# Modulation of layer 2 and both layers' output gates: from TensorE rows to VectorE products with running sums

## Chip, cores and metric

The kernel runs on one core of one Trainium2 chip. The metric is the device time of one execution in microseconds (us), as the median of three runs. TensorE (PE) multiplies matrices into PSUM banks, VectorE (DVE) and ScalarE (ACT) work on them and on SBUF, GpSimd (POOL) does some additions, and SyncE (SP) issues all DMAs. Each engine runs its instructions in the order in which the program lists them.

## What is computed

Two layers of a mixer with shared weights for 128 context tokens and 512 latent tokens, 640 rows of 1024 columns in all. The conditioning vectors (one for each token group) give a shift, a scale and a gate per layer:

```python
for l in range(DEPTH):                                   # DEPTH = 2
    sh, sc, gt = split(silu(c) @ w_mod[l] + b_mod[l], 3) # c_ctx or c; w_mod[l] is 1024 x 3072
    h = rmsnorm(x, pre_w) * (1 + sc) + sh
    proj = h @ w_in                                      # z, xbc, dt | q, k, v, g_b | u, sv, g_c | mg
    y_a = ssd_mixer(...)       # conv, softplus(dt), chunked scans both ways, gated norm
    y_b = diff_attention(...)  # two softmax maps per head
    y_c = chunk_sgmlp(u, sv) * silu(g_c)
    merged = ga * (y_a @ w_branch[0]) + gb * (y_b @ w_branch[1]) + gc * (y_c @ w_branch[2])
    x = x + gt * rmsnorm(merged @ w_out, post_w)
```

## The kernel before

**Dense products.** Every weight matrix is cut into column units. A unit of kind "F" is 128 output columns against all 640 tokens in two halves of 320 (`dense_F`, L532 to L534); a unit of kind "T" is 352, 256 or 512 output columns against five tiles of 128 tokens (`dense_T`, L472 to L474). Both operands are split into a rounded high part and a low part, and three products (high·high, high·low, low·high) are added in PSUM. A weight chunk of 128x1024 is loaded raw by SP (L388), rounded by ACT (L410), and its low part is made by DVE (L419).

**Order.** `schedule()` lists the units of both layers. In each layer come v and gate columns with q and k (attention runs beside them), then mgb (gate of branch b), brb (branch b) mixed with the three sv units, u and gc, two xbc units, mgc and brc in turn, xbc with z (the scans run beside them), mga, bra, and wo (output). All other work is written as small generators. A clock of ticks, one for every six dense products or so, decides when the next piece of each generator is written into the program, so the order on every engine is fixed when the kernel is built. A generator's `yield 3` means "three ticks later".

**PSUM.** Dense halves and tiles take banks of group "d": banks 0 and 1, and, from the end of attention until wo, bank 6 as well. A bank comes free when its result has been read: by ACT for the mg units (L1583), by DVE for brb (L1104), brc (L1107) and bra (L1112), and by a chain ACT, DVE L1020, ACT, DVE L1024 for sv and u.

**Modulation.** Units of kind "M" multiply the conditioning vectors with w_mod: one unit is half of the 1024 rows and 512 columns, four products side by side on 32 columns each (`mod_part`, L666), with the raw weights as the moving operand, in plain float32. There are 24 of them: 8 at the start (scale and shift of layer 1), 8 between the brb units of layer 1 (scale and shift of layer 2), and 4 in bra of each layer (gates, blocks 4 and 5). After two halves `mod_post` adds the bias (L674). Scale and shift are turned into columns by four small products (L683) and finished by L687 and L689. A gate is spread over all 128 partitions by two products with a selecting matrix (L698), and multiplied with the post-norm weight (L700) into `gp`, which `wo_evac` reads (L1467). The post-norm row is spread by a DMA (L661), the bias row loaded by another (L650) into a tile that POOL clears (L649).

**Softplus.** `softplus` (L1168 to L1187) is written in one piece: two ACT instructions and then 18 DVE instructions without a gap, once per layer, while brb ends and u begins.

Of the kernel before, what the change touches and what calls it, by code (L numbers as in the profile page):

```python
# [6 lines left out]
F32 = mybir.dt.float32  # L7
# [3 lines left out]
ALU = mybir.AluOpType  # L11
# [17 lines left out]
D_MOD0, D_MOD, D_GATE = (1, 1), (5, 4), (5, 6)  # L29
D_GAP = (0, 0, 1)  # L30
D_X = (1, 3, 5, 7, 9, 26)
D_MLOAD = 3
# [8 lines left out]
NCOL = 81  # L41
C_PRE, C_CW, C_CB, C_MN, C_DF, C_DB, C_VN, C_HN = 0, 8, 38, 48, 56, 64, 72, 80
# [7 lines left out]
def schedule():  # L50
# [4 lines left out]
    for l in range(DEPTH):  # L55
# [7 lines left out]
        mgb, brb = [("F", "mgb", l, d, 128) for d in range(8)], []  # L63
        for d in range(8):
            brb.append([("F", "brb", l, d, 128)] + ([("M", d % 2, l + 1, d // 2, 512)] if l + 1 < DEPTH else []))
# [8 lines left out]
        for d in range(8):  # L74
            u.append(("F", "mgc", l, d, 128))
            u.append(("F", "brc", l, d, 128))
        for f in range(8):
# [153 lines left out]
class Build:  # L231
    def __init__(self, ctx, tc, a, mem):
        self.a = a
        self.mem = mem
        if tc is None:
            self.nc = self.P = self.PR = self.x1 = Null()
            self.csd = self.ecd = [Null()] * DEPTH
            self.V, self.R, self.I = ([Null()] * 4 for _ in range(3))
        else:
# [14 lines left out]
            self.ecd = [dr.tile([32, 512], F32, name=f"ecd{l}") for l in range(DEPTH)]  # L254
        self.free = [6, 7]
# [8 lines left out]
        for ui, k, kk in chunk_order(self.units):  # L264
            sz = kk * self.units[ui][4]
            self.cid[ui].append(len(self.chunks))
            self.chunks.append((off, sz, self.units[ui][0] == "M"))
# [125 lines left out]
    def mod_load(self, ui):  # L393

        for u in range(ui, min(ui + D_MLOAD + 1, len(self.units))):
            if self.units[u][0] == "M":
# [3 lines left out]
                return  # L400
# [238 lines left out]
    def mod_unit(self, ui):  # L639
        if self.units[ui][1] == 0:  # L640
            self.force(lambda: any(self.group[b] == "s" for b in self.free))
            self.mod_bank = next(b for b in self.free if self.group[b] == "s")
            self.free.remove(self.mod_bank)
        self.mod_part(ui, self.mod_bank)
        self.tick()

# [5 lines left out]
    def mod_part(self, ui, b):  # L652
# [3 lines left out]
        if half == 0:  # L656
            if l or blk >= 4:
                self.mod_bias(l, blk)
            if blk == 4:
                self.pw = self.al(1024)  # L660
                nc.sync.dma_start(out=self.v(self.pw), in_=self.a["postw"][l:l + 1, :].to_broadcast([128, 1024]))  # L661
# [7 lines left out]
        if half:  # L669
            self.go(self.mod_post(l, blk, b, self.rb.pop((l, blk)), D_MOD if l else D_MOD0 if blk < 4 else D_GATE))  # L670

    def mod_post(self, l, blk, b, rb, D):
# [5 lines left out]
        if blk < 4:  # L678
            if l not in self.pm:
                self.pm[l], self.sh[l] = self.al(16), self.al(16)  # L680
            t = (yield from self.take("t")) if l else 5
            for j in range(4):
                nc.tensor.matmul(self.P[:, t, 2 * j:2 * j + 2], self.v(rb, 128 * j, 128), self.msel, start=True, stop=True)  # L683
            yield D[1]
            dst = self.v(self.pm[l], 4 * blk, 4)
            pre = self.v(self.cols[l], C_PRE + 2 * blk, 2).unsqueeze(2).to_broadcast([128, 2, 2])
            nc.vector.scalar_tensor_tensor(out=dst.rearrange("p (j c) -> p j c", j=2), in0=self.P[:, t, 0:4].rearrange("p (j c) -> p j c", j=2),  # L687
                                           scalar=1.0, in1=pre, op0=ALU.add, op1=ALU.mult)
            nc.vector.tensor_copy(self.v(self.sh[l], 4 * blk, 4), self.P[:, t, 4:8])  # L689
            if l or blk == 3:  # L690
                self.give(t)
        else:
            if blk == 4:
                self.gp = self.al(2048)
# [1120 lines left out]
```

## Time and profile before

| what | value |
|---|---|
| median of 3 runs | 2236.98 us (2236.21 to 2237.16) |
| the profiled execution: time, span | 2239.7 us, 2237.7 us |
| PE busy | 2195.2 us, 98% of the span |
| DVE busy | 1371.5 us, 61% |
| ACT busy | 1022.2 us, 46% |
| DMA | 244.05 MB, mean 109 GB/s |
| granted TensorE clock, mean | 0.993 |

The profiled execution is one execution, 2.7 us above the median of the runs. Durations below are from it. Matmul ends are modelled in the profile and matmuls overlap, so what one product costs PE is read from the distance of the starts around it. In the first layer, the units from sv to the last brb stand at 444 to 559 us, u and gc at 560 to 675 us, mgc and brc at about 690 to 804 us, bra at 1023 to 1078 us.

### The profile page before, as it was taken

What the parts mean: (1) busy time and instruction counts of PE and PEld (TensorE: products, weight loads), DVE (VectorE), ACT (ScalarE), POOL (GpSimd) and SP (SyncE); (2) the same over time, 40 slices, a digit from 0 to 9 for tenths busy, and PEclk for the clock granted to TensorE, in tenths of its full rate; (3) what the DMA queues carried; (4) which work ended last, traced back from release to release, by engine and by line L of the source; (5) the groups of instructions that cost most, each with busy time, mean ns of one, the idle gap of its engine ahead of it and who ended that gap; (6) DMA issues with size and microseconds to landing.
All of it is one profiled execution on the core that took longest, in us unless ns stands there. A gap on an engine that the chain in (4) does not pass through costs nothing.

```text
span 2237.7 us, 38780 instructions
## 1 busy us (share of the span) xinstructions
PE 2195.2 (98%) x15482; PEld 2106.5 (94%) x15482; DVE 1371.5 (61%) x2597; ACT 1022.2 (46%) x2242; POOL 186.0 (8%) x196
## 2 busy tenths in 40 slices
PE   7999999999999999999989999999999999999998
PEld 4999999999999999998869999999999999999986
DVE  5476677536554259976375767774464532899654
ACT  4465566432333246762264655564323322677421
POOL 1000000000010113320000000000001011132100
PEclk9999999999999999999999999999999999999999
DMA  8333333234123134633233333322221231545251
GB/s 299 109 100 97 88 102 100 95 116 160 57 77 115 57 104 141 167 118 133 103 128 109 104 88 100 92 81 72 92 81 62 76 116 43 164 132 156 92 189 47
DMA packets 94380, 244.05 MB, mean 109 GB/s; under 512 B 13868, under 2 KB 27244, under 8 KB 94200
## 3 DMA queue, kind: packets, MB, share of 16 engines
q1 hardware_dynamic: 94200, 241.59, 34.5%
q8 instruction: 121, 1.98, 0.4%
q14 instruction: 59, 0.48, 0.1%
HBM read 206.64 MB, written 8.68 MB: 96 GB/s over the span
## 4 chain that ended last, share of the span: by engine, by line
PE 84%; DVE 8%; ACT 4%; issue 2%; DMA 2%; SPq 0%; DVEq 0%; ACTq 0%
PE psum L533 19%; PE psum L534 18%; PE psum L532 18%; PE psum L472 5%; PE psum L473 5%; PE psum L474 5%; PE psum L909 3%; PE psum L956 3%; PE psum L939 1%; PE psum L666 1%; PE psum L1078 1%; ACT plain L923 1%; ACT rounded L410 1%; PE psum L1335 1%; DMA plain<-csd 1%
## 5 line engine op out<-in xcount | busy, mean ns | idle before, releaser
L533 PE MATMUL psum<-shared,rounded 128*128 128x320 f32 x3136 | 972.1, 310 | 4.7 <-DVE shared L1052 4.7
L532 PE MATMUL psum<-shared,rounded 128*128 128x320 f32 x3136 | 973.5, 310 | 0.4 <-DVE plain L1024 0.4
L534 PE MATMUL psum<-shared,rounded 128*128 128x320 f32 x3136 | 965.0, 308 | 0.0
L532 PEld LDWEIGHTS psum<-shared,rounded 128*128 128x128 f32 x3136 | 591.6, 189 | 17.8 <-issue 13.5
L533 PEld LDWEIGHTS psum<-shared,rounded 128*128 128x128 f32 x3136 | 589.8, 188 | 7.2 <-DVE shared L1052 6.1
L534 PEld LDWEIGHTS psum<-shared,rounded 128*128 128x128 f32 x3136 | 591.4, 189 | 0.0
L419 DVE TENSOR_TENSOR rounded<-plain,rounded 128x1024 fp32r<-128x1024 f32 (+2 forms) x226 | 280.1, 1240 | 201.7 <-ACT rounded L410 197.1
L410 ACT CAST rounded<-plain 128x1024 fp32r<-128x1024 f32 (+2 forms) x226 | 235.7, 1045 | 204.3 <-PE psum L533 192.3
L472 PE MATMUL psum<-rounded,shared 128*128 128x256 f32 (+2 forms) x920 | 297.9, 324 | 5.8 <-DVE plain L821 5.8
L473 PE MATMUL psum<-rounded,shared 128*128 128x256 f32 (+2 forms) x920 | 291.7, 317 | 0.2 <-DVE rounded L419 0.2
L474 PE MATMUL psum<-rounded,shared 128*128 128x256 f32 (+2 forms) x920 | 290.9, 316 | 0.9 <-DVE shared L796 0.9
L472 PEld LDWEIGHTS psum<-rounded,shared 128*128 128x128 f32 x920 | 173.4, 188 | 18.7 <-DVE plain L821 7.4
L474 PEld LDWEIGHTS psum<-rounded,shared 128*128 128x128 f32 x920 | 173.5, 189 | 10.6 <-DVE shared L796 1.5
L473 PEld LDWEIGHTS psum<-rounded,shared 128*128 128x128 f32 x920 | 173.4, 188 | 9.5 <-DVE rounded L419 0.9
L917 DVE TENSOR_REDUCE plain<-psum 128x1 f32<-128x640 f32 (+1 forms) x160 | 107.7, 713 | 87.2 <-PE psum L909 86.1
L923 ACT ACTIVATE plain<-psum,plain 128x640 f32<-128x640 f32 (+1 forms) x160 | 112.3, 711 | 4.1 <-DVE plain L917 2.7
L909 PE MATMUL psum<-shared 128*128 128x320 f32 (+1 forms) x576 | 99.8, 312 | 0.0
L1583 ACT ACTIVATE plain<-psum 128x320 f32<-128x320 f32 x96 | 41.6, 436 | 123.3 <-PE psum L534 117.7
L962 ACT ACTIVATE plain<-psum,plain 128x128 f32<-128x128 f32 x80 | 29.6, 370 | 135.3 <-PE psum L956 96.4
L1018 ACT ACTIVATE plain<-psum 128x320 f32<-128x320 f32 (+1 forms) x62 | 27.7, 447 | 128.1 <-PE psum L534 65.2
L909 PEld LDWEIGHTS psum<-shared 128*128 128x128 f32 x576 | 84.6, 189 | 0.7 <-ACT plain L923 0.4
L956 PE MATMUL psum<-plain 128*128 128x128 f32 x640 | 81.3, 274 | 0.0
(268 smaller groups left out, 2558.0 us busy)
## 6 DMA issues: line engine op xcount, KB each, us to landing
plain<-in_wp_dram SPq DMA_DIRECT2D x250, 512.0 KB, 4.3
shared<-in_wp_dram SPq DMA_DIRECT2D x42, 512.0 KB, 6.4
shared<-csd SPq DMA_DIRECT2D x36, 320.0 KB, 5.2
shared<-shared SPq DMA_DIRECT2D x64, 160.0 KB, 3.1
plain<-csd SPq DMA_DIRECT2D x28, 320.0 KB, 7.1
plain<-plain SPq DMA_DIRECT2D x128, 64.0 KB, 2.0
plain<-in_wp_dram SPq DMA_DIRECT2D x12, 528.0 KB, 7.4
shared<-shared SPq DMA_DIRECT2D x32, 192.0 KB, 2.6
```

The lines of the kernel that those rows point to most:

```text
L410: self.nc.scalar.copy(self.r(blk[0], 0, sz), self.v(self.w_raw[i], 0, sz))
L419: self.nc.vector.tensor_tensor(out=self.r(blk[1], 0, sz), in0=self.v(raw, 0, sz), in1=self.v(blk[0], 0, sz), op=ALU.subtract)
L472: mm(out, ht, wh, start=(k == 0), stop=False)
L473: mm(out, ht, wl, start=False, stop=False)
L474: mm(out, lt, wh, start=False, stop=(k == KD - 1))
L532: mm(out, wh, xh, start=(k == 0), stop=False)
L533: mm(out, wh, xl, start=False, stop=False)
L534: mm(out, wl, xh, start=False, stop=(k == KD - 1))
L909: mm(self.P[:, ss[m] + half, 0:n], self.r(H["q"], 1280 * i + 640 * m + 128 * t, 128), k, start=(i == 0), stop=(i == 1))
L917: nc.vector.tensor_reduce(out=self.v(st, m, 1), in_=src[m], op=ALU.max, axis=AX.XY if t else AX.X, negate=True)
L923: nc.scalar.activation(pv, src[m], AF.Exp, bias=self.v(st, m, 1), accum_out=self.v(st, 2 + m, 1))
L956: mm(out, self.v(wt, 128 * j, 128), self.v(H["v"], 128 * ((j + 1) % 5), 128), start=(j == 0), stop=(j == 4))
```

## The change

Eight M units at the start stay. The 16 others go, with their bias rows, the small products L683 of layer 2, the spreading products L698 and the postw row. In their place stand 32 units of kind "V", all of them in layer 1 of the program: each is one tile of 128 columns of w_mod, **transposed**, so that a partition is an output column and the 1024 inputs lie along the row. `mod_tile` multiplies the tile with the conditioning row, spread over the partitions, once for each of the two vectors, as a DVE scalar_tensor_tensor of 128x1024 that also writes the sum of the row (`accum_out`). 12 of the 32 are placed between the second brb and the first u unit, 20 among the mgc and brc units. V units load one tile of 512 KB each through SP, ahead of the unit before or the one before that. The bytes of w_mod loaded are the same.

`cond_rows` loads and spreads the two conditioning rows once (2 x 512 KB) and applies the SiLU: two ACT and two DVE instructions of 128x1024. `mod_end` adds the bias, forms 1+scale and gate times post-norm weight on tiles of 16 to 48 columns, transposes the 16 gate columns of each layer on PE, and writes them to DRAM. `gate_rows` reads them back, spread over 128 partitions (2 x 512 KB per layer), two bra units ahead of wo. The softplus gets gaps of one or two ticks between its steps.

```diff
-        for d in range(8):
-            brb.append([("F", "brb", l, d, 128)] + ([("M", d % 2, l + 1, d // 2, 512)] if l + 1 < DEPTH else []))
+        brb = [[("F", "brb", l, d, 128)] for d in range(8)]
+        vs = [("V", "mod", v // 24, v % 24, 128) for v in range(16, 48)] if l == 0 else []
...
+        for lo, hi, part in ((len(u) - 16, len(u), vs[V_N:]), (start + V_AT, names.index("u", start), vs[:V_N])):
+            for j, v in reversed(list(enumerate(part))):
+                u.insert(lo + (j + 1) * (hi - lo) // len(part), v)
...
             u.append(("F", "bra", l, d, 128))
-            if 3 <= d <= 6:
-                u.append(("M", (d - 3) % 2, l, 4 + (d - 3) // 2, 512))
...
+    def cond_rows(self):
...
+        for c in range(2):
+            nc.sync.dma_start(out=self.v(cb, 1024 * c, 1024), in_=self.a["crow"][c:c + 1, :].to_broadcast([128, 1024]))
...
+            nc.scalar.activation(self.v(th), x, AF.Tanh, scale=0.5)
+            yield 3
+            nc.vector.scalar_tensor_tensor(out=x, in0=self.v(th), scalar=1.0, in1=x, op0=ALU.add, op1=ALU.mult)
...
+    def mod_tile(self, ui):
...
+        yield from self.until(lambda: self.condok)
+        jb = self.al(1024)
+        for c in range(2):
+            nc.vector.scalar_tensor_tensor(out=self.v(jb if c == 0 else wb), in0=self.v(wb), scalar=1.0, in1=self.v(self.cb, 1024 * c, 1024),
+                                           op0=ALU.mult, op1=ALU.mult, accum_out=self.v(self.mc[l], 2 * i + c, 1))
+            if c == 0:
+                self.fr(jb)
+                yield 3
...
+            nc.tensor.transpose(self.P[0:16, t, 0:128], self.v(gt), self.ident)
...
+            nc.sync.dma_start(out=self.gd[l].rearrange("c (j n) -> (c j) n", n=128), in_=self.v(gr, 0, 128, 0, 16))
...
+    def gate_rows(self, l):
+        self.gp = self.al(2048)
+        for c in range(2):
+            self.nc.sync.dma_start(out=self.v(self.gp, 1024 * c, 1024), in_=self.gd[l][c:c + 1, :].to_broadcast([128, 1024]))
...
         nc.vector.tensor_scalar(d, e, 2.0, None, op0=ALU.add)
+        yield 2
         nc.vector.reciprocal(d, d)
+        yield 1
...
         for c in (11, 9, 7, 5, 3):
+            yield 1
             nc.vector.tensor_tensor(out=p, in0=p, in1=s, op=ALU.mult)
...
         while self.units[ui][1] != "wo":
+            if self.units[ui][3] == 6:
+                self.gate_rows(l)
             run_unit(ui)
...
-        self.force(lambda: self.mods[l] >= {4, 5})
```

The order of the instructions shows it at three places. On PE, between the fourth brb unit of layer 1 (L534 ends it) and the third sv unit (L472 begins it), the kernel before has a half M unit, four products on 32 columns:

```order
L533 MATMUL psum<-shared_398,rounded 128x320
L534 MATMUL psum<-shared_398,rounded 128x320
L666 MATMUL psum<-plain 32x512 x4
L472 MATMUL psum<-rounded,shared_65 128x352
L473 MATMUL psum<-rounded,shared_65 128x352
```

and the changed kernel, where the same three dense lines are L537 to L539 and L477 to L479, has

```order
L538 MATMUL psum<-shared_400,rounded 128x320
L539 MATMUL psum<-shared_400,rounded 128x320
L477 MATMUL psum<-rounded,shared_65 128x352
L478 MATMUL psum<-rounded,shared_65 128x352
L479 MATMUL psum<-rounded,shared_65 128x352
```

The M products are gone and nothing stands in their place. The same holds at all 16 units, 4 groups of L683 and 8 products L698, and apart from the two transposes L744 no other product on PE has changed its place among the dense ones.

On DVE, while brb 5 of layer 1 is computed (L1061 begins the layer norm of sv, L1104 frees a bank of brb, L419 is a weight's low part, the 128x5 rows are the norm's inverse root), the kernel before has

```order
L549 TENSOR_SCALAR plain<-plain 128x5
L556 TENSOR_TENSOR plain<-plain 128x5
L559 TENSOR_TENSOR plain<-plain 128x5
L562 SCALAR_TENSOR_TENSOR plain<-plain 128x5
L1104 SCALAR_TENSOR_TENSOR plain<-plain,psum 128x320
L556 TENSOR_TENSOR plain<-plain 128x5
```

and the changed kernel, where they are L554 to L567, L1156 and L424, has

```order
L711 SCALAR_TENSOR_TENSOR plain<-plain 128x1024 x2
L424 TENSOR_TENSOR rounded<-plain,rounded 128x1024
L1113 TENSOR_SCALAR plain<-plain 128x5
L552 TENSOR_SCALAR plain<-plain 128x5
L553 TENSOR_SCALAR plain<-plain 128x5
L554 TENSOR_SCALAR plain<-plain 128x5
L561 TENSOR_TENSOR plain<-plain 128x5
L711 SCALAR_TENSOR_TENSOR plain<-plain 128x1024 x2
L564 TENSOR_TENSOR plain<-plain 128x5
L1156 SCALAR_TENSOR_TENSOR plain<-plain,psum 128x320
```

Four products with sums (L711) now stand ahead of the instruction that frees the first bank of brb 5.

On SP, in bra of layer 1, the kernel before loads bias rows, the post-norm row and gate weights between the last branch weights and the input rows (L1453):

```order
L388 DMA plain<-in_wp_dram 128x1024 x9
L650 DMA plain<-in_bmod_dram 1x512
L661 DMA plain<-in_postw_dram 128x1024
L388 DMA plain<-in_wp_dram 128x1024 x6
L650 DMA plain<-in_bmod_dram 1x512
L388 DMA plain<-in_wp_dram 128x1024 x4
L1453 DMA plain<-in_xin_dram 128x1024 x5
```

and the changed kernel, where they are L393 and L1509, has

```order
L393 DMA plain<-in_wp_dram 128x1024 x9
L758 DMA plain<-gd_73 128x1024 x2
L393 DMA plain<-in_wp_dram 128x1024 x2
L1509 DMA plain<-in_xin_dram 128x1024 x5
```

The two gate rows (L758) take the place of eleven loads, and stand ahead of the last weights and the input rows.

## Rows read from the trace of the kernel before

**Rows 1.** The page, part 1: busy time, share of span, instructions

```profile
PE 2195.2 (98%) x15482; PEld 2106.5 (94%) x15482; DVE 1371.5 (61%) x2597; ACT 1022.2 (46%) x2242; POOL 186.0 (8%) x196
```

**Rows 2.** Timeline of PE around an M unit and L683: start, us, instruction

```profile
534.76 0.31 PE L534 MATMUL psum<-shared,rounded 128*128 128x320 f32 x1
535.00 1.06 PE L666 MATMUL psum<-plain 128*32 128x512 f32 x8
...
536.25 0.31 PE L533 MATMUL psum<-shared,rounded 128*128 128x320 f32 x1
...
540.32 0.31 PE L534 MATMUL psum<-shared,rounded 128*128 128x320 f32 x1
540.47 0.95 PE L683 MATMUL psum<-plain 128*128 128x2 f32 x8
...
541.51 0.30 PE L533 MATMUL psum<-shared,rounded 128*128 128x320 f32 x1
```

**Rows 3.** Timeline of PE around a spreading product L698 in bra

```profile
1056.08 0.31 PE L534 MATMUL psum<-shared,rounded 128*128 128x320 f32 x1
1056.23 1.02 PE L698 MATMUL psum<-plain 128*128 128x512 f32 x2
...
1057.23 0.31 PE L533 MATMUL psum<-shared,rounded 128*128 128x320 f32 x1
```

**Rows 4.** Lines L666, L683, L698 after 400 us: records, duration ns min/median/max

```profile
L666 PE MATMUL psum<-plain x128: 592/605/618, 434.6 to 2164.8; 128*32 128x512 f32 x128
L683 PE MATMUL psum<-plain x32: 165/251/251, 448.7 to 558.4; 128*128 128x2 f32 x32
L698 PE MATMUL psum<-plain x16: 592/593/593, 1056.2 to 2173.7; 128*128 128x512 f32 x16
```

**Rows 5.** Timeline of PE around two transposes of 128x128

```profile
697.62 0.31 PE L534 MATMUL psum<-shared,rounded 128*128 128x320 f32 x1
697.76 0.27 PE L1218 MATMUL psum<-plain 128*128 128x128 f32 x1
...
698.13 0.31 PE L533 MATMUL psum<-shared,rounded 128*128 128x320 f32 x1
```

**Rows 6.** Busy us by stretch: PE, PEld, DVE, ACT, POOL; clock, DMA share, GB/s

```profile
690.00:804.00 114.00, 114.00 (x792) 113.36 (x791) 35.46 (x43) 25.25 (x40) 12.45 (x15) 1.00 0.22 76
499.50:558.60 59.10, 59.10 (x403) 54.95 (x400) 36.07 (x79) 12.73 (x21) 3.83 (x3) 1.00 0.42 151
```

**Rows 7.** DVE instructions by shape: busy us, mean ns; idle before

```profile
L419 DVE TENSOR_TENSOR rounded<-plain,rounded 128x1024 fp32r<-128x1024 f32 x208 | 259.7, 1250 | 194.4 <-ACT rounded L410 189.9 <-DMA plain<-in_wp_dram 4.5
L930 DVE SCALAR_TENSOR_TENSOR plain<-plain 128x640 f32<-128x640 f32 x64 | 56.7, 885 | 2.3
L1481 DVE SCALAR_TENSOR_TENSOR plain<-plain 128x1024 f32<-128x1024 f32 x9 | 11.6, 1285 | 0.3
L1476 DVE TENSOR_SCALAR plain<-plain 128x1 f32<-128x1 f32 x10 | 1.5, 154 | 0.3
```

**Rows 8.** DVE instructions by shape, 499 to 560 us

```profile
L1535 DVE BATCH_NORM_STATS2 plain<-plain 128x6 f32<-128x512 f32 x10 | 6.4, 681 | 0.0
```

**Rows 9.** Timeline of DVE: two sv tiles, two brc units

```profile
480.61 0.52 DVE L1020 SCALAR_TENSOR_TENSOR plain<-plain,psum 128x352 f32<-128x352 f32 x1 [2.23 <-ACT plain L1018]
...
484.46 0.52 DVE L1020 SCALAR_TENSOR_TENSOR plain<-plain,psum 128x352 f32<-128x352 f32 x1 [2.24 <-ACT plain L1018]
...
745.21 0.49 DVE L1107 SCALAR_TENSOR_TENSOR plain<-plain,psum 128x320 f32<-128x320 f32 x1 [0.83 <-PE psum L534]
...
759.07 0.49 DVE L1107 SCALAR_TENSOR_TENSOR plain<-plain,psum 128x320 f32<-128x320 f32 x1 [0.83 <-PE psum L534]
```

**Rows 10.** The page, part 6, DMA issues: count, KB each, median us to landing

```profile
plain<-in_wp_dram SPq DMA_DIRECT2D x250, 512.0 KB, 4.3
...
plain<-in_xin_dram SPq DMA_DIRECT2D x7, 512.0 KB, 8.8
```

**Rows 11.** Timeline of PE in layer 2, behind the softplus

```profile
1664.31 0.42 PE L532 MATMUL psum<-shared,rounded 128*128 128x320 f32 x1 [0.44 <-DVE plain L1024]
```

More of the change, by code (lines that the diff above doesn't have):

```diff
@@ L254, in __init__ @@
             self.ecd = [dr.tile([32, 512], F32, name=f"ecd{l}") for l in range(DEPTH)]
+            self.gd = [dr.tile([2, DM], F32, name=f"gd{l}") for l in range(DEPTH)]
         self.free = [6, 7]
@@ L266, in __init__ @@
             self.cid[ui].append(len(self.chunks))
-            self.chunks.append((off, sz, self.units[ui][0] == "M"))
+            self.chunks.append((off, sz, self.units[ui][0] in ("M", "V")))
             off += 128 * sz
@@ L677, in mod_post @@
         yield D[0]
[L678 to L694, printed above, removed]
-            o = 512 * (blk - 4)
-            for c in range(2):
-                t = yield from self.take("t")
-                nc.tensor.matmul(self.P[:, t, :], self.gsel[c], self.v(rb), start=True, stop=True)
-                yield 3
-                nc.vector.tensor_tensor(out=self.v(self.gp, 1024 * c + o, 512), in0=self.P[:, t, :],
-                                        in1=self.v(self.pw, o, 512), op=ALU.mult)
-                self.give(t)
-            if blk == 5:
-                self.fr(self.pw)
@@ new lines, in mod_post @@
+        if l not in self.pm:
+            self.pm[l], self.sh[l] = self.al(16), self.al(16)
+        t = 5
+        for j in range(4):
+            nc.tensor.matmul(self.P[:, t, 2 * j:2 * j + 2], self.v(rb, 128 * j, 128), self.msel, start=True, stop=True)
+        yield D[1]
+        dst = self.v(self.pm[l], 4 * blk, 4)
+        pre = self.v(self.cols[l], C_PRE + 2 * blk, 2).unsqueeze(2).to_broadcast([128, 2, 2])
+        nc.vector.scalar_tensor_tensor(out=dst.rearrange("p (j c) -> p j c", j=2), in0=self.P[:, t, 0:4].rearrange("p (j c) -> p j c", j=2),
+                                       scalar=1.0, in1=pre, op0=ALU.add, op1=ALU.mult)
@@ new lines, in mod_tile @@
+    def mod_tile(self, ui):
+        nc = self.nc
+        kind, name, l, i, n = self.units[ui]
+        wb = self.w_raw.pop(self.cid[ui][0])
+        yield from self.until(lambda: self.condok)
[6 more added lines that the diff above has]
+                yield 3
+        self.fr(wb)
+        self.nv += 1
+        if self.nv == 32:
+            self.fr(self.cb)
+            self.go(self.mod_end(), 1)
@@ L1540, in evac_sv @@
                     yield 4
-                    self.softplus(l)
+                    yield from self.softplus(l)
                     self.dtok = True
@@ L1646, in layer @@
         nc.gpsimd.tensor_scalar(self.v(self.bs), self.v(self.bs), 0.25, None, op0=ALU.mult)
-        while self.units[ui][1] in ("u", "gc"):
+        while self.units[ui][1] in ("u", "gc", "mod"):
             run_unit(ui)
@@ L1652, in layer @@
         self.force(lambda: self.dtok)
-        run_unit(ui)
-        run_unit(ui + 1)
-        ui += 2
+        while ("x", 9) not in state:
+            run_unit(ui)
+            ui += 1
         self.go(self.ssd_prep(l, state.pop(("x", 8)), state.pop(("x", 9))), 2)
```

100 lines of the change are left out of this document (71 added, 29 removed).

## The prediction

> **What bounds the kernel now.** I read the busy shares first: PE is busy for 98% of the span and DVE for 61% [rows 1]. A busy PE is only a hint, since its matmul ends are modelled; so next I took the stretches in which the change takes something away or puts something in. In the 59 us from the third sv unit to the last brb, and in the 114 us of mgc and brc, PE is busy for every microsecond and the clock stands at its full level, while DVE works 36 of 59 us and 35 of 114 us [rows 6]. There PE sets the pace and DVE has time left: 23 us and 78 us. Whatever leaves PE's queue there is time off the kernel, as long as DVE, which frees PE's banks, does not become late.
>
> **What leaves PE.** A matmul's price is what it does to the starts around it. L534 starts at 534.76, then comes a half M unit, and the second dense product behind it (L533) starts at 536.25 [rows 2]. Dense products of 320 columns follow each other every 0.145 us (two brc units of 48 products each take 759.07 - 745.21 = 13.86 us, so 6.93 us a unit [rows 9]); without M that L533 would have started at 534.76 + 2 x 0.145 = 535.05. So a half M unit costs 1.20 us. The same reckoning for a group of L683 gives 541.51 - 540.32 - 0.29 = 0.90 us [rows 2], and for one L698 1057.23 - 1056.08 - 0.29 = 0.86 us [rows 3]. How many go: each of these float32 products leaves two records. The 128 records of L666 after 400 us are 64 products, four to a half unit: 16 half units. The 32 of L683 are 4 groups of four, the 16 of L698 are 8 products [rows 4]. The sum is 16 x 1.20 + 4 x 0.90 + 8 x 0.86 = 19.2 + 3.6 + 6.9 = **29.7 us**. None of it stood in a wait: on both sides the dense products run at their own distance, so nothing else is uncovered when it goes. The order of PE is otherwise unchanged, so that no product gets an earlier or later neighbour.
>
> **What is added to PE.** Two transposes of 16 columns. Two transposes of 128 columns moved the second dense start from 697.91 to 698.13 [rows 5], 0.2 us together; standing apart they may cost 0.2 each. I take **+0.4 us** (0.2 to 0.6).
>
> **The products on DVE.** 64 of them, 128x1024 with a running sum. No row of before has a DVE instruction that also writes a sum. The nearest is the same instruction without the sum: L1481, 1285 ns [rows 7]. If writing the sum costs a further small instruction, the 128x1 rows give 154 ns [rows 7], 1.44 us in all. I take 1.36 us, midway: 87 us of DVE work, and 2 x 1.3 us to prepare the conditioning rows; 4 L674, 8 small ones and the gates' L700 leave, which is little. Now by stretch:
>
> - *mgc and brc:* 40 products are 54 us. 35.5 + 54 = 90 of 114 us. DVE keeps 24 us, 3.0 us for each mgc/brc pair. A brc bank must be free two halves (6.9 us) after it is full, as three banks go round, so that even two products ahead of L1107 do no harm. Cost nothing; the cover is that slack.
> - *sv 0 to brb 3:* 12 products. Counted from the order with the trace's durations, the other work is 24 us; 24 + 16 = 40 of 52 us. Cost nothing.
> - *sv 2 to brb 7:* this is the tight one. In the new order, PE takes 19.3 us for the sv unit (five tiles, one every 3.85 us by L1020 [rows 9]) and 4 x 6.93 for the brb units, 47 us. DVE has the eight weight parts, ten BN instructions of 681 ns [rows 8], the evacuations and five passes of the layer norm, 33.5 us, and now 14 products, 19 us: 52.5 us in 47. Ledger from the end of the fourth sv tile, where DVE waits for PE in the old trace: until the first half of brb 5 is read, DVE has 13.9 us of other work (four weight parts 4.9, six BN 4.1, the rest 4.9), six products 8.2 us, the reading itself 0.5 and one wait for ACT 0.5: 23.0 us. PE needs that bank after 3.85 + 6.93 + 3.47 + 6.93 = 21.2 us. PE waits 1.8 us. Continued to the u halves (six more products, three weight parts, then softplus steps), another 0.9 us. I take **+2.7 us**. The lower end is 0: consecutive DVE rows overlap by nearly 0.1 us, which over 30 instructions takes the lateness away. The upper end is 6 us, if the products run at 1.44 us and the transfers below add a wait or two.
>
> **The transfers.** As many bytes as before. A V tile is loaded one dense unit (6.93 us) or more ahead and lands in 4.3 us by the median of such loads [rows 10]; it is hidden. A late tile would hold all of DVE's queue, the low weight parts and the bank readings behind it (the first rival). The conditioning rows go ahead of about 4.8 us of sv; ACT waits for them with sv's evacuation behind it, up to 4 us if they take the 8.8 us of the slowest 512 KB loads [rows 10]; a sv bank has 7.7 us for a chain of some 2.5 us, so this is hidden, and would cost a few tenths if not. The gate rows are asked for two bra units (13.9 us) ahead of wo, in SP's queue before the last weights and the input rows; two loads of 512 KB at 4.3 to 8.8 us stay within that and the first wo tile. They stand in place of eleven loads, so what is queued behind them is not worse off. Cost nothing.
>
> **Softplus in pieces.** In layer 2 the old block made PE wait once, 0.44 us [rows 11]; that goes: **-0.4 us**. In layer 1 it takes its 6.5 us of DVE out of the tight stretch into u and gc, which have time; that is already in the ledger.
>
> **The sum.** 2239.7 (the profiled execution) - 29.7 + 0.4 + 2.7 - 0.4 = 2212.7 us. That execution was 2.7 us above the median, so the forecast for the median is **2210 us**, -1.2%.
>
> **The rivals.**
>
> *1. DVE stands at tiles that have not landed.* Weight loads and V tiles now share mgc and brc. If tiles take the 8.8 us of the slowest loads, DVE waits 1.9 us at each, 2.5 tiles a pair: 4.7 us against 3.0 us of slack, so 1.7 us a pair, 14 us in eight pairs: **2224 us**. Against it: these stretches moved 76 and 151 GB/s [rows 6], far from busy. Between 2215 and 2230 I give this and a somewhat larger wait in the tight stretch 10%.
>
> *2. The products run at half rate: slower than before.* L930 and L1481 differ by 384 columns and 400 ns [rows 7], 1.04 ns a column and 0.22 us fixed. At two passes a column a product takes 2.35 us, and with the writing of the sum 2.50. Then mgc and brc ask 35.5 + 100 = 135.5 us of DVE in 114, PE waits 21.5 us; sv 2 to brb 7 asks 68.5 us, with one bank round (6.9 us) to give, 14.5 us; sv 0 to brb 3 another 2. Together 38 us where I have 2.7: **2245 us**. The gain is eaten from a product of about 2.4 us on. For it: no row of before has the running sum. Against it: with the two float32 sources and without the sum the instruction takes 1285 ns for 1024 columns, as the plain two-source L419 does in 1250 [rows 7]. [...] I give it 6%.
>
> *3. No wait at all in the tight stretch.* Then 2207.3 us, and less where the removed rows cost more than I reckon at the changes of shape: **2204 to 2208**, 14%.
>
> That the M products are not really gone is excluded by the order.
>
> **Chances.** Forecast (2208 to 2215) 70%, rival 3 14%, rival 1 10%, rival 2 6%. The range from 2204 to 2224 leaves out the far half of rival 1 and all of rival 2, 11%, and some 5% for durations that no row shows. About 0.2% (4.5 us) is what a measurement can tell from no change: faster 0.91, same 0.04 (rival 2 with a product near 2.4 us), slower 0.05.
>
> **What would show it.** L666 has 64 records, all before 60 us, no L698, and the stretch from the first brb to u is 13 us shorter, less what PE waits there. The products have a mean of 1.29 to 1.44 us. PE's waits name DVE L1156 or L1076 (brb, u) with 1 to 5 us in all, and none in mgc and brc. DVE's waits for V tiles are below 5 us in sum. bra is some 8 us shorter in each layer. I am wrong if the products take over 2 us, or if PE shows idle time in mgc and brc, or if wo waits for the gate rows.

## The result and the profile after

The changed kernel takes **2209.47 us** (median of 4 runs, 2208.56 to 2210.12), the kernel before 2236.60 us beside it (4 runs, 2235.17 to 2237.16): ratio 0.9879, 95% interval 0.9862 to 0.9896. It is 27 us, 1.2%, faster. The profiled execution of the changed kernel took 2209.23 us, its span is 2207.2 us.

The page of the changed kernel, part 1 (answers to [rows 1]):

```profile
PE 2165.7 (98%) x15308; PEld 2096.1 (95%) x15308; DVE 1437.1 (65%) x2709; ACT 1023.1 (46%) x2246; POOL 189.7 (9%) x188
```

PE is 29.5 us shorter and has 174 instructions less; DVE is 65.6 us longer. The span fell by 30.5 us, about as much as PE's busy time. The medians of the timed runs differ by 27.1 us, less than the two traces, because the traced execution of the kernel before was a longer one than its median; the table below is from the two traces.

**Where it went.** Both kernels run 12288 dense products (three lines each: L532, L533, L534 and their sisters before, L537, L538, L539 and theirs after) in the same order. So each start can be set against the start of the same product in the other trace:

| stretch | shift of the starts at its end, after minus before (us) | change in the stretch |
|---|---|---|
| up to the first brb of layer 1 | -0.6 (-0.7 at the first dense product) | |
| brb and sv of layer 1, up to the first gc unit | -13.9 | -13.4 |
| u, gc, mgc, brc, xbc, z, mga, up to the second bra unit of layer 1 | -13.6 | +0.4 |
| the rest of bra, into the first wo unit | -22.0 | -8.4 |
| up to the second bra unit of layer 2 | -22.9 | -1.0 |
| the rest of bra, into the first wo unit | -31.3 | -8.4 |
| up to the last product | -30.8 | +0.5 |

The steps inside stand where a unit left PE: -1.2 at a half M unit, -2.1 at a half M unit with an L683 group. At the place of [rows 2], where L534, L532 and L533 started at 534.76, 536.00 and 536.25, the changed kernel's PE timeline (start, us, instruction) has

```profile
526.30 0.31 PE L539 MATMUL psum<-shared,rounded 128*128 128x320 f32 x1
526.44 0.30 PE L537 MATMUL psum<-shared,rounded 128*128 128x320 f32 x1
526.58 0.31 PE L538 MATMUL psum<-shared,rounded 128*128 128x320 f32 x1
```

In mgc and brc, which took 40 products, nothing is lost: the shift is -14.1 at the first mgc unit and at the end of the last brc. Around 1665 us (layer 2's softplus) stands a step of -0.6.

**The products.** Line L711 of the changed kernel, which is the product with the running sum: count, then duration in ns (shortest, median, longest), first and last start, shape.

```profile
L711 DVE SCALAR_TENSOR_TENSOR plain<-plain x63: 1210/1219/1896, 452.2 to 793.4; 128x1024 f32<-128x1024 f32 x63
L711 DVE DVE_READ_ACCUMULATOR plain<-plain x63: 73/82/86, 453.3 to 794.6; 128x1 f32 x63
```

Each product is two records: the product, and a short one that reads the sum. (The 64th, with the same durations, is listed apart.) All 64 have a mean of 1250 ns: three, at 708, 736 and 764 us, took 1896 ns, the 61 others at most 1227 ns. What ran beside these three is told in the last section. The next view is DVE's timeline of the same kernel at brb 5: start, us, instruction.

```profile
526.22 1.22 DVE L711 SCALAR_TENSOR_TENSOR plain<-plain 128x1024 f32<-128x1024 f32 x1
527.36 0.08 DVE L711 DVE_READ_ACCUMULATOR plain<-plain 128x1 f32 x1
527.36 1.22 DVE L711 SCALAR_TENSOR_TENSOR plain<-plain 128x1024 f32<-128x1024 f32 x1
528.51 0.08 DVE L711 DVE_READ_ACCUMULATOR plain<-plain 128x1 f32 x1
528.51 0.16 DVE L564 TENSOR_TENSOR plain<-plain 128x5 f32<-128x5 f32 x1
528.59 0.48 DVE L1156 SCALAR_TENSOR_TENSOR plain<-plain,psum 128x320 f32<-128x320 f32 x1
...
546.92 0.49 DVE L1076 SCALAR_TENSOR_TENSOR plain<-plain,psum 128x320 f32<-128x320 f32 x1 [0.54 <-ACT plain L1074]
```

The reading record starts with the next instruction: from one product to the next are 1.14 us, not 1.22 + 0.08. L1156 (it reads a bank of brb) ends at 529.07, L1076 (it reads a bank of u) at 547.41. The next two rows are PE's timeline at the products that need these two banks:

```profile
529.91 0.30 PE L537 MATMUL psum<-shared,rounded 128*128 128x320 f32 x1
...
550.71 0.30 PE L537 MATMUL psum<-shared,rounded 128*128 128x320 f32 x1
```

They run in step with the products ahead of them. The first bank was free 0.8 us early, the second 3.3 us. PE waits for DVE at no brb and no u. From 455 to 560 us and from 690 to 830 us it has no wait at all. Its largest waits in the whole trace (line waiting, what it waits for: us, times, longest) are other ones, which the kernel before has too, with 11.8, 5.8 and 4.7 us:

```profile
PE psum L792 <- DVE plain L768: 9.0, 1, 9.0
PE psum L477 <- DVE plain L873: 5.6, 8, 1.2
PE psum L538 <- DVE shared L1104: 5.4, 4, 1.9
```

Busy time by stretch in the changed kernel (columns as in [rows 6]), for the two stretches that hold the products:

```profile
455.00:560.00 105.00, 105.00 (x699) 105.00 (x698) 83.76 (x163) 31.60 (x51) 4.51 (x2) 1.00 0.42 143
690.00:793.00 103.00, 103.00 (x714) 102.37 (x713) 71.07 (x103) 21.64 (x30) 20.25 (x18) 1.00 0.50 174
```

PE is busy throughout at the full clock, and DVE, at 80% and 69%, still keeps 21 and 32 us.

### The profile page after: what moved, and what is told of

Same layout as the page of the kernel before. It is cut to its first block, busy times and chain, and to the rows that moved or that the text cites. A ratio compares the mean times of both kernels' runs of the same rounds, so it can differ in the third digit from the quotient of the medians.

```text
span 2207.2 us, 38531 instructions
## 1 busy us (share of the span) xinstructions
PE 2165.7 (98%) x15308; PEld 2096.1 (95%) x15308; DVE 1437.1 (65%) x2709; ACT 1023.1 (46%) x2246; POOL 189.7 (9%) x188
## 4 chain that ended last, share of the span: by engine, by line
PE 83%; DVE 8%; ACT 4%; issue 3%; DMA 1%; SPq 0%; POOL 0%; DVEq 0%; ACTq 0%; POOLq 0%
PE psum L538 19%; PE psum L539 18%; PE psum L537 18%; PE psum L477 5%; PE psum L478 5%; PE psum L479 5%; PE psum L961 3%; PE psum L1008 3%; PE psum L991 1%; DMA shared<-csd 1%; ACT rounded L415 1%; PE psum L1130 1%; ACT plain L975 1%; PE psum L1391 1%; DVE rounded L424 1%
## 5 line engine op out<-in xcount | busy, mean ns | idle before, releaser
L538 PE MATMUL psum<-shared,rounded 128*128 128x320 f32 x3136 | 971.1, 310 | 5.5 <-DVE shared L1104 5.4
L537 PE MATMUL psum<-shared,rounded 128*128 128x320 f32 x3136 | 968.9, 309 | 0.0
L539 PE MATMUL psum<-shared,rounded 128*128 128x320 f32 x3136 | 963.4, 307 | 0.0
L537 PEld LDWEIGHTS psum<-shared,rounded 128*128 128x128 f32 x3136 | 590.7, 188 | 5.4 <-issue 4.1
L538 PEld LDWEIGHTS psum<-shared,rounded 128*128 128x128 f32 x3136 | 589.0, 188 | 6.9 <-DVE shared L1104 6.8
L539 PEld LDWEIGHTS psum<-shared,rounded 128*128 128x128 f32 x3136 | 590.3, 188 | 0.0
L424 DVE TENSOR_TENSOR rounded<-plain,rounded 128x1024 fp32r<-128x1024 f32 (+1 forms) x223 | 276.5, 1241 | 160.1 <-ACT rounded L415 160.0
L415 ACT CAST rounded<-plain 128x1024 fp32r<-128x1024 f32 (+1 forms) x223 | 232.5, 1045 | 191.3 <-PE psum L538 160.0
L477 PE MATMUL psum<-rounded,shared 128*128 128x256 f32 (+2 forms) x920 | 297.4, 323 | 5.6 <-DVE plain L873 5.6
L479 PE MATMUL psum<-rounded,shared 128*128 128x256 f32 (+2 forms) x920 | 291.6, 317 | 0.3 <-DVE shared L848 0.3
L477 PEld LDWEIGHTS psum<-rounded,shared 128*128 128x128 f32 x920 | 173.8, 189 | 15.9 <-DVE plain L873 7.2
L479 PEld LDWEIGHTS psum<-rounded,shared 128*128 128x128 f32 x920 | 173.8, 189 | 10.5 <-DVE shared L848 1.0
L1014 ACT ACTIVATE plain<-psum,plain 128x128 f32<-128x128 f32 x80 | 29.5, 369 | 135.5 <-PE psum L1008 96.5
L1706 POOL TENSOR_SCALAR plain<-plain 128x1024 f32<-128x1024 f32 x2 | 6.8, 3380 | 978.2 <-DMA plain<-in_bs_dram 493.0
```

What stands on the lines that cost most here:

```text
L415: self.nc.scalar.copy(self.r(blk[0], 0, sz), self.v(self.w_raw[i], 0, sz))
L424: self.nc.vector.tensor_tensor(out=self.r(blk[1], 0, sz), in0=self.v(raw, 0, sz), in1=self.v(blk[0], 0, sz), op=ALU.subtract)
L477: mm(out, ht, wh, start=(k == 0), stop=False)
L479: mm(out, lt, wh, start=False, stop=(k == KD - 1))
L537: mm(out, wh, xh, start=(k == 0), stop=False)
L538: mm(out, wh, xl, start=False, stop=False)
```

## The experiments

Where nothing else is said, each is the changed kernel with the edit shown. Times are medians; the ratio is against the kernel before, measured beside it.

| label | time (us) | ratio, 95% interval |
|---|---|---|
| changed kernel | 2209.47 | 0.9879 (0.9862 to 0.9896) |
| e1_short | 2208.66 | 0.9874 (0.9859 to 0.9889) |
| e2_twice | 2242.72 | 1.0030 (1.0019 to 1.0040) |
| e3_late | 2210.12 | 0.9881 (0.9864 to 0.9897) |
| e3_lead1 | 2210.23 | 0.9878 (0.9862 to 0.9895) |
| e4_block | 2210.41 | 0.9888 (0.9873 to 0.9903) |
| e5_vn8 | 2213.92 | 0.9889 (0.9875 to 0.9904) |
| e5_vn16 | 2234.05 | 0.9982 (0.9972 to 0.9991) |
| e5_vn16l1 | 2219.01 | 0.9915 (0.9898 to 0.9931) |
| g2_guard | 2238.31 | 1.0002 (0.9993 to 1.0011) |
| g5_guard | 2209.86 | 0.9872 (0.9857 to 0.9887) |
| e7_mtwice (from the kernel before) | 2244.09 | 1.0029 (1.0020 to 1.0039) |
| b_again (the kernel before) | 2238.16 | 1.0001 (0.9990 to 1.0011) |

### Do the products cost anything? (e1_short)

```diff
-nc.vector.scalar_tensor_tensor(out=self.v(jb if c == 0 else wb), in0=self.v(wb), ..., in1=self.v(self.cb, 1024 * c, 1024),
+nc.vector.scalar_tensor_tensor(out=self.v(jb if c == 0 else wb, 0, 16), in0=self.v(wb, 0, 16), ..., in1=self.v(self.cb, 1024 * c, 16),
```

> Every one of the 64 products works on 16 columns instead of 1024; all loads, waits and orders stay (the sums of layer 2's scale and shift and of both gates then come from 16 columns alone). It takes some 64 us of work off VectorE, 24 products of it out of the stretch from sv2 to brb7 of layer 1. Theory A (the products are hidden; none of them sets the end of a TensorE wait): the time is that of the changed kernel, 2209.5 us, within 1.5 us, and the dense products' places in the trace do not move. Rival B (the ledger of the prediction: 2.7 us of waits in the tight stretch are paid somewhere in the changed kernel): 2206.8 us. Rival C (VectorE delays TensorE at many places by little): 2200 us or less.

Measured 2208.66 us, the same as the changed kernel. In the trace no dense product stands more than 0.9 us from its place in the changed kernel's, and the last one 0.3 us. The two stretches, as above:

```profile
455.00:560.00 105.00, 105.00 (x699) 105.00 (x698) 61.80 (x161) 31.65 (x51) 4.10 (x2) 1.00 0.40 143
690.00:793.00 103.00, 103.00 (x714) 102.37 (x713) 34.29 (x105) 21.50 (x30) 12.81 (x18) 1.00 0.49 176
```

DVE has 22 and 37 us less to do, and PE does exactly what it did. So the products are hidden in full; a cheaper product would bring nothing.

### How far does the cover reach? (e2_twice)

```diff
+for last in range(2):
+    jb = None if c and last else self.al(1024)
     nc.vector.scalar_tensor_tensor(out=self.v(wb if jb is None else jb), in0=self.v(wb), ...
```

> Every product is done twice, the second into the same running sum's place, so that the result stays the same; VectorE gets 64 further instructions of 1.145 us from start to start, 73 us. Theory A (VectorE hides the products only as far as its idle time and the slack of the banks reach): in layer 1 from sv2 to brb7 24 more products are 27.5 us against some 6 us of idle time and 3.3 us of slack at u's first bank, so some 18 us of TensorE waits there; in mgc and brc 40 more are 46 us against 32 us of idle time in the stretch, some 14 us of waits. In all 25 to 35 us, 2235 to 2245 us. Rival B (the products cost nothing because VectorE is idle for 35% of the span): 2209.5 us. Rival C (each product is paid in full): 2209.5 + 73 = 2283 us.

Measured 2242.72 us: 33 us more, within theory A, and slower than the kernel before. PE's waits from 455 to 580 us and from 690 to 840 us (the edit moves lines by two: L1158 is L1156, L1078 is L1076, L746 the transpose of the gates' sums):

```profile
PE psum L537 <- DVE plain L1158: 6.7, 2, 6.1
PE psum L537 <- DVE plain L1078: 4.2, 2, 2.9
PE psum L477 <- DVE plain L1078: 1.8, 2, 1.2
PE psum L477 <- DVE plain L1158: 1.1, 1, 1.1
...
PE psum L537 <- DVE plain L1161: 6.7, 3, 4.0
PE psum L746 <- DVE plain L736: 2.8, 1, 2.8
```

They name the two banks of the prediction's ledger, brb's and u's, and then brc's (L1161). Against the changed kernel the dense products fall back by 20 us up to 577 us and by another 14 us in mgc, brc and behind them, near the expected 18 and 14. Up to 577 us 15.9 us stand at eight waits, less than the 18 expected, and 4.3 us in 35 products that start further apart behind them (the granted clock was 0.96 on the mean from 455 to 580 us). Of 73 us of added DVE work 40 were hidden.

### Must the tiles be loaded ahead? (e3_late, e3_lead1)

```diff
-D_MLOAD, V_AT, V_N = 2, 10, 12
+D_MLOAD, V_AT, V_N = 0, 10, 12    # e3_late; 1, 10, 12 in e3_lead1
```

> The tile of transposed weights is loaded at its own unit instead of up to two units ahead, so each pair of products waits on VectorE for a transfer that takes about 3.9 us. Theory A (VectorE's queue runs behind in the tight stretch, so the tile has landed before its product's turn comes; in mgc and brc one wait of 2 to 4 us per tile meets 32 us of idle time over 20 tiles): 0 to 6 us more, 2209.5 to 2215.5 us, and the added idle time before the products is under 60 us in all. Rival B (the accounting of the prediction's rival 1: every late tile is paid for beyond a slack of 3 us a pair): 11 us more, 2221 us.

Measured 2210.12 us, no difference that can be told. DVE's waits for the tiles in e3_late, from 455 to 560 us and from 690 to 800 us:

```profile
DVE plain L711 <- DMA plain<-in_wp_dram: 6.4, 5, 1.9
...
DVE plain L711 <- DMA plain<-in_wp_dram: 10.2, 6, 2.8
```

The waits are there, 17 us, with all of DVE's queue behind them. In mgc and brc PE waits for none of it. In the crowded stretch the dense products lose 3.9 us, of which 1.9 us are left by the end of the trace; from 690 to 840 us they lose less than 0.1 us. Rival 1 of the prediction expected a stop at each of the 20 tiles in mgc and brc, 38 us in all, and allowed 3.0 us a pair, 24 us, for nothing. Here 6 stops of 10.2 us stay within that, so this run does not test its price beyond the slack. e3_lead1 came last, to settle a question of e5_vn16l1:

> The changed kernel, 12 tiles ahead of u, each tile loaded at most one unit ahead instead of two; the planner's 15 steps stay. It tells what of the 9.5 us of the 16 tiles with this lead belongs to the lead and what to the four further tiles. Theory A (a lead of one unit is enough, the 9.5 us are the 8 further products, 9.2 us, paid in full): 2209.5 us within 1 us. Rival B (the shorter lead makes about 3.6 us of it in the same stretch and the tiles the 5.9 us of the slack ledger): 2213 us.

Measured 2210.23 us; DVE waits 0.5 us for one tile, and the dense products move by 0.4 us in the stretch. With 12 tiles a lead of one unit is enough.

### Softplus in one piece (e4_block)

```diff
 nc.vector.tensor_scalar(d, e, 2.0, None, op0=ALU.add)
-yield 2
 nc.vector.reciprocal(d, d)
-yield 1
...
```

> The changed kernel with the softplus of dt in one piece again: 18 VectorE instructions of 6.7 us in a row at the start of u, where the units of layer 1 find VectorE 3.3 us ahead of the bank that TensorE needs next. Theory A (with the products in place, the pieces are needed): a TensorE wait of about 3 us in layer 1 and the old one of 0.4 to 0.6 us in layer 2, 2213 us. Rival B (the pieces matter only in layer 2, as the trace of before shows it): 0.5 us more, 2210 us.

The median, 2210.41 us, is 0.9 us above the changed kernel, which the intervals don't tell apart. Theory A's 2213 us was not measured, and rival B's 2210 us was. Yet the trace has the waits of theory A, the first one shorter than its 3 us: 1.9 us at u in layer 1 and 0.4 us in layer 2. PE's timeline in layer 1:

```profile
553.61 0.41 PE L537 MATMUL psum<-shared,rounded 128*128 128x320 f32 x1 [1.86 <-DVE plain L1076]
553.86 0.31 PE L538 MATMUL psum<-shared,rounded 128*128 128x320 f32 x1
...
554.84 0.47 PE L537 MATMUL psum<-shared,rounded 128*128 128x320 f32 x1
555.11 0.47 PE L538 MATMUL psum<-shared,rounded 128*128 128x320 f32 x1
555.38 0.47 PE L539 MATMUL psum<-shared,rounded 128*128 128x320 f32 x1
```

Soon behind the wait the products start 0.27 us apart instead of 0.145, for some 13 of them; against the changed kernel they are 3.7 us late by 559 us, 2.0 from the wait and 1.7 from the slower products. From 50 us on that execution stood 2.6 us ahead of the changed kernel's (from 29 to 35 and from 35 to 41 us it was granted a clock of 1.00, the other 0.60 and 0.83), so that its end is only 1.0 us later. So by the trace the pieces are worth 3.7 us where the products made the stretch tight, more than the 0.4 us that the trace of before could show; the medians neither bear this out nor speak against it.

### More or fewer tiles ahead of u (e5_vn16, e5_vn8)

```diff
-D_MLOAD, V_AT, V_N = 2, 10, 12
+D_MLOAD, V_AT, V_N = 2, 10, 16    # e5_vn16; 2, 10, 8 in e5_vn8
```

> 16 of the 32 tiles, instead of 12, have their place between brb0 and u of layer 1; the other 16 stay in mgc and brc. That puts 8 more products of 1.145 us, 9.2 us, on VectorE where the changed kernel has it without idle time from 511 to 547 us. Theory A (the slack there is used up: 3.3 us at u's first bank, 0.9 us at the bank of brb5): a TensorE wait of 9.2 - 3.3 = 5.9 us, about 2215 us, unless the added tiles fall into the 6 us of idle time ahead of 511 us, which brings it down to some 3 us, 2212.5 us. Rival B (VectorE still has room): 2209.5 us.

Measured 2234.05 us: 24.6 us more, far outside theory A. In the stretch the theory holds: from 455 to 575 us the dense products lose 5.9 us. But 7 us are lost before 60 us, where no tile has been touched, and the rest in many steps of 0.5 to 2 us in attention and the scan. PE's waits of e5_vn16, first the one up to 70 us that the changed kernel does not have, then those from 480 to 575 us:

```profile
PE psum L657 <- DMA plain<-in_wp_dram: 3.7, 1, 3.7
...
PE psum L537 <- DVE plain L1076: 2.1, 3, 1.3
PE psum L537 <- DVE plain L1156: 1.2, 2, 0.9
PE psum L537 <- DVE plain L1059: 0.8, 1, 0.8
```

> 8 of the 32 tiles, instead of 12, have their place between brb0 and u of layer 1, and 24 stand in mgc and brc. Theory A (nothing is paid in either stretch of the changed kernel, and mgc and brc have 32 us of VectorE idle time for 9.2 us more): 2209.5 us within 1.5 us, VectorE busy 80 us of the 103 us of mgc and brc. Rival B (the loads of the tiles or VectorE are already at their limit in mgc and brc): 3 us or more on top, 2212.5 us.

Measured 2213.92 us, by the ratios (0.9889 against 0.9879) not told apart from the changed kernel, though its median is 4.5 us higher beside a kernel before that was 0.9 us slower. No step over 0.4 us stands between 455 and 800 us, which is theory A; its last product is 2.8 us late, from small steps in attention and the scan, where no tile stands.

### The memory planner's distance (g2_guard, g5_guard, e5_vn16l1)

Ahead of 60 us e5_vn16 has the same instructions in the same order as the changed kernel. What differs is the placement. The planner in the kernel looks for each buffer's place so that the buffers ahead of it and behind it there are some allocation steps away, and takes a smaller distance for a buffer that finds none. It begins with the largest of 15, 10, 5, 2 and 0 with which everything fits in the end. That is 15 for the kernel before and the changed one, 5 for e5_vn8 and 2 for e5_vn16. It is a distance tried first, no guarantee: of the changed kernel's 1890 buffers the plan lets 78 follow another within fewer than 5 steps, against 571 with 2.

```diff
-D_PLAN = (3, 0)
+D_PLAN = (6, 0)    # g2_guard, begins with 2; (5, 0) in g5_guard, begins with 5
```

> The changed kernel, instruction for instruction in the same order, with one number of the memory planner changed: two buffers may follow each other in one place of the on-chip memory from 2 allocation steps apart, instead of 15. With 16 tiles ahead of u the planner finds room only with 2. Theory A (closer reuse lets loads and producers wait for the last reader of the place, and this made most of the 24 us that 16 tiles cost): about 17 us, 2226 us, with some 7 us of it ahead of 60 us, where TensorE waited for a weight transfer, and the rest in many waits of about 1 us; nothing of it in the stretch from sv2 to u. Rival B (the 24 us come from the tiles, the placement is worth nothing): 2209.5 us.

Measured 2238.31 us: this one number costs 29 us and takes the whole gain away. Its largest losses are 7.0 us before 60 us and 6.8 us at 819 us; from 455 to 560 us it loses 0.3 us. PE's waits of g2_guard, the one up to 75 us that the changed kernel does not have, and that from 800 to 830 us:

```profile
PE psum L657 <- DMA plain<-in_wp_dram: 3.6, 1, 3.6
...
PE psum L744 <- DVE plain L734: 5.3, 1, 5.3
```

And DVE's largest wait from 800 to 821 us:

```profile
DVE plain L734 <- DMA gd<-plain: 8.5, 1, 8.5
```

The last line shows the mechanism at 819 us. L734 writes layer 2's 16 gate columns; what it waits for is the transfer of layer 1's gate rows (L751, issued on SP's queue at 812.93 behind eight loads of the scan), which reads a buffer of its own. The two only meet if they have the same place, one after the other, and in this plan they do: both buffers begin at column 2432 of the first pool, the second three allocation steps behind the first, while the changed kernel's plan has them at 2128 and 2112. DVE stops for 8.5 us, and PE's transpose L744 waits for it. The other losses, some 13 us in many steps, were not followed to their buffers.

> The same with 5 allocation steps, as the planner needs for 8 tiles ahead of u. Theory A (placement made the 2 to 4 us that 8 tiles cost over 12): 2 to 4 us more, 2212 to 2213 us. Rival B: 2209.5 us.

Measured 2209.86 us, as the changed kernel: beginning with 5 steps is enough (75 buffers follow another within fewer than 5), rival B. The small loss of e5_vn8, if there is one, is not the number; it stays open.

> 16 tiles ahead of u, each loaded at most one unit ahead instead of two, so that the planner keeps its 15 steps. Theory A (8 more products on a VectorE without idle time, 9.2 us against 3.3 us of slack at u's first bank; the placement made the rest of the 24 us): about 6 us of TensorE waits between brb4 and u, 2215.5 us. Rival B (the tiles themselves made the 24 us): 2230 us or more. Rival C (the tiles cost nothing, the placement all): 2209.5 us.

Measured 2219.01 us. The 15 steps gave back 15 of e5_vn16's 24.6 us, so rival B falls; what remains lies wholly between 465 and 570 us, where the dense products lose 11.7 us (1.9 us come back later). That is over the 5.9 us of theory A. The largest of DVE's waits from 455 to 560 us:

```profile
DVE plain L711 <- DMA plain<-in_wp_dram: 9.9, 5, 3.1
```

e5_vn16, with the same tiles at the same places and a lead of two units, has no such wait and lost 5.9 us there; e3_lead1, with this lead and 12 tiles, has 0.5 us of it. So theory A's price of the tiles stands where they come in time, 5.9 us. Of the 11.7 us, 8.6 stand in six steps at PE's waits, and 3.1 in 24 products that start further apart behind them (last section). That the waits are longer than in e5_vn16 fits tiles that come late: with 16 in the same stretch they follow each other more closely, and a lead of one unit no longer covers every transfer. No run tests this apart.

### What a half M unit costs (e7_mtwice)

```diff
+n = 2 if half == 0 and (l or blk >= 4) else 1
+for again in range(n):
+    for j in range(4):
         nc.tensor.matmul(self.P[32 * j:32 * j + 32, b, :], ..., start=(half == 0), stop=(half == 1 or again < n - 1))
```

> The kernel before, with the first half's four products of each of the eight modulation blocks behind the start (layer 2's scale and shift, both gates) done twice; the second pass overwrites the first, so the result stays the same. Eight half units more. Theory A (TensorE sets the time wherever the M units stand, each half unit is worth its 1.20 us in full): 8 x 1.20 = 9.6 us more than the kernel before. Rival B (part of it falls into time in which TensorE would have waited, and the units were worth less): 5 us or less.

Measured 2244.09 us beside 2237.54, ratio 1.0029: 6.5 us, between the two theories. PE's timeline of e7_mtwice at one doubled unit:

```profile
524.94 0.31 PE L534 MATMUL psum<-shared,rounded 128*128 128x320 f32 x1
525.18 1.92 PE L666 MATMUL psum<-plain 128*32 128x512 f32 x16
527.04 0.42 PE L532 MATMUL psum<-shared,rounded 128*128 128x320 f32 x1
527.29 0.31 PE L533 MATMUL psum<-shared,rounded 128*128 128x320 f32 x1
```

Sixteen records take 1.92 us where eight took 1.06 [rows 2], so the second pass costs 0.86, and 8 x 0.86 = 6.9 us. The 1.20 us of a whole half unit hold 0.86 of products and 0.34 that the second pass did not pay again; most of it stands where PE leaves the dense products and comes back to them (0.24 us up to the unit and 0.25 us behind it, where dense products are 0.145 apart), the rest inside. In the trace, against the kernel before, each of the eight doubled units is a step of 0.86 us in the dense products' starts. All of it is paid for in full; only the split was not known.

### The kernel before once more (b_again)

> The kernel before once more, for a second profile. The first was 2239.7 us, 2.7 us over the median of the timed runs. Theory A (the surplus lies ahead of the first dense product, where TensorE waits for VectorE and the first loads, and differs from execution to execution): in this profile the dense products stand against each other as in the first to within 0.3 us from the first to the last, and only the common start has moved, by up to 4 us. Rival B (the surplus is spread over the kernel): the distance grows along the trace.

Its profiled execution took 2238.88 us. The first dense product starts 1.0 us sooner than in the first trace and the last 0.9 us, with up to 0.8 us of difference from that in between: theory A for these two executions, though not to within 0.3 us. So the pair does not show where the 2.7 us are. The times of this kernel go with the granted clock: on record are 13 executions with a mean clock of 0.993, which took 2239.2 us on the mean, and 18 with 0.996, which took 2235.7 us; the first profile had 0.993. One place where executions differ is the start. From 29 to 35 and from 35 to 41 us the first profile was granted 0.62 and 0.81, this one 0.52 and 0.91, and e7_mtwice, with the same units there, 1.00 in both: its dense products, 1.5 us ahead at the first, were 3.5 us ahead at 40 us. But the changed kernel's profile had a low clock there too (0.60 and 0.83) and did not stand above its median. What made up the 2.7 us stays open.

## Why the prediction was right

**The sign and the 2210 us** were right, and so was the reason: PE sets the pace, what leaves its queue is time off the kernel, and DVE hides what it takes over. Point by point:

- *What leaves PE, 29.7 us.* Right. The shift of the dense products grows by 30.1 us from the first to the last: 13.4 us in brb (8 x 1.20 + 3.6 = 13.2 by the prediction), and 8.4 us in each of the two bra stretches (8.2 each). Pricing a unit by the starts around it, and not by its duration, was what made this exact: e7_mtwice shows that over a quarter of the price is not paid for the products themselves.
- *The transposes, +0.4.* Right in size: L744 stands in the dense sequence at 0.1 us each, 0.2 us together, the prediction's lower end.
- *The product, 1.36 us.* Over-priced: 1.14 us from start to start. There is a second instruction, as the upper bound supposed, but it is 82 ns, not 154, and lies under the next one. Rival 2 (2.35 us and more) falls. With the sum and two float32 sources in SBUF the product took 1219 ns by the median, no longer than the form without a sum, 1285 [rows 7]; the half rate was the rival's estimate, and no run shows it.
- *The wait in the tight stretch, +2.7.* **This step failed**: it measured 0. The ledger set 23.0 us of DVE work against 21.2; in the trace the first bank came 0.8 us early instead of 1.8 late, so 2.6 us less. Six products at 1.36 instead of 1.14 are 1.3 us of it. The rest is the other work, 14.9 us in the ledger: in the trace, from the fourth sv tile at 508.9 us to the end of L1156 at 529.07, the 28 other rows have durations of 14.2 us, but from start to start they and 0.8 us of idle time fill only 13.3 us. Consecutive DVE rows started there before the one ahead had ended (L424 at 517.16 us took 1.22 us, and the next row started at 518.30); the prediction named this overlap for its lower end and left it out of the sum. The place was right: e2_twice waits at just these two banks, and e5_vn16 lost 5.9 us where 9.2 us of products less 3.3 us of slack make 5.9.
- *Softplus, -0.4.* The step at layer 2 is -0.6. That the pieces also keep the tight stretch free of a wait was in the ledger, and e4_block shows it.
- *Transfers, 0.* Right: no DVE wait for a tile in the changed kernel, no wait of PE at wo for the gate rows. Rival 1 did not come, as no tile was late; e3_late shows only that stops within its slack are free.
- *The offset, -2.7.* **Wrong too.** The changed kernel's profiled execution was 0.2 us below its median. The profiled time came out at 2209.2 where the steps gave 2212.7, and the median at 2209.5 where they gave 2210: the wait that was not there and the offset that was not there cancelled, and that is luck. By its mechanism the result is rival 3 (no wait); the forecast had its time for a partly wrong reason. Of the marks that the prediction named, the mean of a product (1.29 to 1.44 us expected, 1.25 measured) and the 1 to 5 us of waits on L1156 and L1076 were missed, the others met.

## What to carry to other kernels

Here work moved from an engine that set the pace to one with idle time was worth its full price by the starts around it (29.7 us priced, 30.1 us measured), until a bank's slack on the receiving engine was used up: 64 products cost no time, and 64 more cost 33 us. Add up a queue by the distance of starts and not by durations. When such a change needs more buffers, ask what the placement gives up: a planner that begins with a distance of 2 steps instead of 15 took back the whole gain without moving one instruction.

## What the runs showed of the hardware

- The sum that a DVE product writes cost nothing that can be seen: 1219 ns for 1024 columns with it, 1285 without [rows 7], an 82 ns reading that overlapped the next instruction, 1.14 us from start to start.
- Products and GpSimd's additions took longer side by side. L1162 adds 128x320 in SBUF and took 0.75 to 0.89 us in the kernel before (there L1110) and in e1_short; in the changed kernel eight of them, each beside a product, took 1.66 to 1.80 us. The three products of 1896 ns started while such an addition ran, at 708.42, 736.15 and 763.89 us. DVE and POOL of the changed kernel, and then POOL of e1_short:

```profile
707.28 1.22 DVE L711 SCALAR_TENSOR_TENSOR plain<-plain 128x1024 f32<-128x1024 f32 x1
707.44 1.80 POOL L1162 TENSOR_TENSOR plain<-plain 128x320 f32<-128x320 f32 x1 [2.33 <-DVE plain L1159]
708.42 1.90 DVE L711 SCALAR_TENSOR_TENSOR plain<-plain 128x1024 f32<-128x1024 f32 x1
...
707.30 0.88 POOL L1162 TENSOR_TENSOR plain<-plain 128x320 f32<-128x320 f32 x1 [2.59 <-DVE plain L1159]
```

  With the products cut to 16 columns POOL is busy for 12.81 us from 690 to 793 us, with the whole products for 20.25. The time did not change, since PE waited for neither.
- Behind some PE waits the products ran slower. In e4_block a wait of 1.9 us was followed by products at 0.27 us instead of 0.145 (granted clock 0.93 on the mean from 540 to 566 us, 1.00 in the changed kernel), 3.7 us in all. In e5_vn16l1 a wait of 3.5 us that ended at 526.4 us was followed by products at 0.27 us too, and the granted clock was 0.84 in the 12 us behind it:

```profile
516.00:528.00 12.00, 8.54 (x54) 8.28 (x54) 8.88 (x16) 3.12 (x5) 0.00 (x0) 0.87 0.77 270
528.00:540.00 12.00, 12.00 (x73) 12.00 (x72) 11.76 (x30) 1.06 (x1) 0.00 (x0) 0.84 0.44 161
```

  In e5_vn16, where no wait of the same stretch was over 1.3 us, the granted clock was 1.00 on the mean from 455 to 575 us. The bounds of the prediction priced a wait at its own length only.
